# Low weight parts of gate and up, the scale product and sums of squares on VectorE instead of GpSimd

## The chip, the cores and the metric

The kernel runs on one core of one Trainium2 chip. The metric is the device time of one execution in microseconds (us). The core's engines are named as the profile names them: PE is TensorE, DVE is VectorE, ACT is ScalarE, POOL is GpSimd, and SP issues DMAs. PEld is PE's loading of weights, which overlaps its matmuls. Each engine works through its own list of instructions in order; between engines there are semaphores.

## The reference

Two layers of an encoder trunk over 1040 tokens (16 meta tokens and 1024 of the sequence), width 1024, all in float32:

```python
for l in range(DEPTH):                                   # DEPTH = 2
    h = h + hybrid_mixer(rmsnorm(h, norm1_w[l]), ...)    # ends with mix @ w_out
    h = h + swiglu(rmsnorm(h, norm2_w[l]), w_gate_up[l], w_down[l])
h = rmsnorm(h, final_norm_w)

def swiglu(h, w_gate_up, w_down):
    gate, up = jnp.split(h @ w_gate_up, 2, axis=-1)
    return (jax.nn.silu(gate) * up) @ w_down
```

D_FF is 2816, which is 22 tiles of 128 columns. The mixer (a chunked gated delta rule in both directions and a short convolution) is not touched here, apart from the output projection `mix @ w_out` that ends it. rmsnorm needs the sum of squares of h over the 1024 channels for each token, and these sums are gathered while the output projection is being made.

## The kernel before

**Layout.** The residual stream lies channels-first: eight tiles of 128 channels by 1040 tokens. Matmuls take the weights as the stationary operand, 128 by 128, and stream 260 tokens (layer 0, which needs 1040) or 512 tokens (layer 1, which needs only the last 1024).

**Split operands.** To come near float32 with the faster fp32r matmul, every operand is split into a high part, rounded to fp32r by an ACT copy, and a low part, the difference. One product then takes three matmuls: high by high, high by low, low by high (lines 1015 to 1017 in gate and up, 157 to 159 in the plain dense layers, 1435 to 1437 in down). Weights are split on the chip each time: a DMA brings 128x512 raw values, ACT writes `hi` (line 997), and a subtraction writes `lo` (line 998):

```python
def w_op(src, early=False):                                              # L993
    hi, lo = wslot(early)
    ...
    act(out=hi, in_=src, func=AF.Copy)                                   # L997
    ptt(out=lo, in0=src, in1=hi.bitcast(F32), op=ALU.subtract)           # L998
```

`tt` is an elementwise operation of two tensors on DVE, `ptt` the same on POOL. `wslot` hands out seven pairs of buffers in turn, one for each of the products of a round; a pair is free again when PE has ended the product that read it.

**Gate and up.** For each of the 22 tiles f there is one round of the loop at line 1280. It makes a 2x2 block product in the manner of Strassen and Winograd, with seven products in place of eight. Weight operands: A11, A12, A21, A22 are loaded, and four DVE instructions make sums of them (lines 1290, 1291, 1294, 1295), which gives S1 to S4. Each of the seven operands goes through `w_op`. The sums on the side of the tokens (T1 to T4) are made once a layer, with lines 965, 977 and 178. The products p1 to p7 are added up in PSUM banks, and DVE empties these at lines 1314 (p5), 1325 and 1328 (p3, p6), 1332 (p7) and 1341 (p4); ACT empties p1 and p2 (lines 1310 and 1337). Products 5 and 3 share a bank, and so do 6, 7 and 4: the next product may add to the bank only after DVE has read the one before. Layer 0 does each product in two halves of 260 tokens, layer 1 in one of 512. For the first four tiles, the products with A11 and A12 are made early (`early_part`, line 1041), while the output projection ends. At the end of a round the scale of rmsnorm (`rv`, the reciprocal root for each token) is multiplied on, and silu and the product follow:

```python
ptt(out=gv, in0=gv, in1=rv, op=ALU.mult)        # L1355
tt(out=uv, in0=uv, in1=rv, op=ALU.mult)         # L1356
act(out=gv, in_=gv, func=AF.Silu)               # L1357
row_done = tt(out=uv, in0=uv, in1=gv, op=ALU.mult)   # L1358
```

The row goes to DRAM, and sums of rows and of weights for the down stage are prepared in between (lines 1360 and 1364).

**Output projection, second part.** `out_part(z, m)` (line 941) makes the delta-rule half of the projection for channel tile m and token half z, adds it to the residual (line 905, on DVE), and adds the squares to the row of sums: ACT squares (line 949), and line 950 adds. Its weights are split in `wsplit` (line 131) on POOL at this place. When all eight tiles are in, four small matmuls (line 207) sum over the channels.

**Order.** The program is written in plain order with priorities, and a scheduler that keeps a timeline by its own costs arranges each engine's list when the kernel is built. An instruction that changes engine or cost can therefore move others, also on other engines.

Of the kernel before, what the change touches and what calls it, by code (L numbers as in the profile page):

```python
# [7 lines left out]
F32 = mybir.dt.float32  # L8
# [3 lines left out]
ALU = mybir.AluOpType  # L12
# [30 lines left out]
def trunk(ctx: ExitStack, tc: tile.TileContext, xT, w_in, w_ba, w_out, w_gu, w_dn,  # L43
# [21 lines left out]
    def c4k(tag="c"):  # L65
        return sb.tile([128, L], F32, tag="c", bufs=2, name=nm(tag))
# [33 lines left out]
    tt = nc.vector.tensor_tensor  # L100
    stt = nc.vector.scalar_tensor_tensor
    ts = nc.vector.tensor_scalar
    ptt = nc.gpsimd.tensor_tensor
# [29 lines left out]
    def wload(src, nk):  # L133

        res = []
        step = min(nk, WK)
        for k0 in range(0, nk, step):
            kk = min(step, nk - k0)
            hi = wp.tile([128, WK, 128], F32R, tag="whi", name=nm("whi"))
            lo = wp.tile([128, WK, 128], F32R, tag="wlo", name=nm("wlo"))  # L140
            wsplit(src[:, k0:k0 + kk, :], hi[:, 0:kk, :], lo[:, 0:kk, :])
            for k in range(kk):
                res.append((hi[:, k, :], lo[:, k, :]))
        return res

    def dense(ws, xs, chunks, evac, pool=None):

        for (n0, n1) in chunks:
            n = n1 - n0
            ps = (pool or pacc)()  # L150
            K = len(xs)
            here = tc.cur_priority
            if mmp[0] is not None:
                at_prio(mmp[0])
            for k in range(K):
                (wh, wl), (xh, xl) = ws[k], xs[k]
                mm(ps[:, :n], wh, xh[:, n0:n1], start=(k == 0), stop=False)  # L157
                mm(ps[:, :n], wh, xl[:, n0:n1], start=False, stop=False)  # L158
                mm(ps[:, :n], wl, xh[:, n0:n1], start=False, stop=(k == K - 1))  # L159
            if mmp[0] is not None:  # L160
                mmp[0] = tc.cur_priority
                at_prio(here)
            here = tc.cur_priority
            if evp[0] is not None:
                at_prio(evp[0])
            evac(ps[:, :n], n0, n1)
            if evp[0] is not None:
                evp[0] = tc.cur_priority
                at_prio(here)
            for q in (jobs, jobs2, jobs3):  # L170
                f = q.pop(0) if q else None
                if f is not None:
                    f()
# [106 lines left out]
    for l in range(DEPTH):  # L280
# [622 lines left out]
        def add_h(m, then=None):  # L903
            def f(ps, n0, n1):
                tt(out=hr[m][:, n0:n1], in0=ps, in1=hr[m][:, n0:n1], op=ALU.add)
                if then is not None:
                    then(n0, n1)
            return f
# [23 lines left out]
        def half(ap, z):  # L932

            v = ap.rearrange("p (g e) -> p g e", g=4) if len(ap.shape) == 2 else ap.rearrange("p k (g e) -> p k g e", g=4)
            s = slice(1, 3) if z == 0 else slice(0, 4, 3)
            return v[:, s, :] if len(ap.shape) == 2 else v[:, :, s, :]
# [4 lines left out]
        def out_part(z, m):  # L941
            dense(wload(w_out[l, m, :, 0:4, :], 4), os_, hcut[z], add_h(m), pwide)

            v, sv = half(hr[m][:, o0:L], z), half(ss[:, o0:L], z)
            if m == 0:
                act(out=sv, in_=v, func=AF.Square)
            else:
                sq = c4k("sq")[:, 0:NB].rearrange("p (g e) -> p g e", g=2)
                act(out=sq, in_=v, func=AF.Square)
                (ptt if z == 1 and m % 2 == 0 else tt)(out=sv, in0=sv, in1=sq, op=ALU.add)  # L950
            for (n0, n1) in hcut[z]:
                dma(hd[m][:, n0:n1], hr[m][:, n0:n1])

# [39 lines left out]
        def w_op(src, early=False):  # L993
            hi, lo = wslot(early)
            n = src.shape[1]
            hi, lo = hi[:, 0:n, :], lo[:, 0:n, :]
            act(out=hi, in_=src, func=AF.Copy)  # L997
            ptt(out=lo, in0=src, in1=hi.bitcast(F32), op=ALU.subtract)  # L998
            return hi, lo

        bn = [0]
# [278 lines left out]
        for f in range(FT):  # L1280
            A11, A12, A21, A22 = raw4("raw"), raw4("raw"), raw4("ck2"), raw4("ck2")
            dma(A11, w_gu[l, f, 0, :, 0:4, :])
            dma(A21, w_gu[l, f, 1, :, 0:4, :])
            dma(A22, w_gu[l, f, 1, :, 4:8, :])
            dma(A12, w_gu[l, f, 0, :, 4:8, :])
            s1t, s2t = raw4("ck2"), raw4("ck2")
            W = {}
            if f >= NE:
                W["A11"] = w_op(A11)
            tt(out=s1t, in0=A21, in1=A22, op=ALU.add)  # L1290
            tt(out=s2t, in0=s1t, in1=A11, op=ALU.subtract)
            W["S1"] = w_op(s1t)
            W["S2"] = w_op(s2t)
            tt(out=s2t, in0=A12, in1=s2t, op=ALU.subtract)  # L1294
            tt(out=A21, in0=A11, in1=A21, op=ALU.subtract)
            end = f == FT - 1
            for n, a in ([("S3", A21), ("A22", A22), ("S4", s2t), ("A12", A12)] if end else
                         [("S4", s2t), ("S3", A21), ("A12", A12), ("A22", A22)]):
                if f >= NE or n != "A12":
                    W[n] = w_op(a)  # L1300
            adds = s_under(f)
            g, u = early[f] if f < NE else (row((X[1], Y[1])[f % 2] + "f"), row(X[1], F32, 3))
            ps = {}


            def p1(j):
                ps["a", j], ps["c", j], ps["b", j] = pbank(), pbank(), pbank()
                if f >= NE:
                    prod(ps["a", j], W["A11"], T["B11"], j, True)
                    act(out=part(u, 0, j), in_=pin(ps["a", j]), func=AF.Copy)  # L1310

            def p5(j):
                prod(ps["c", j], W["S1"], T["T1"], j, True)
                tt(out=part(u, 1, j), in0=pin(ps["c", j]), in1=part(u, 0, j), op=ALU.add)

            def p3(j):
                prod(ps["c", j], W["S4"], T["B22"], j, False)
                (gadd if end else gset)(ps["c", j], j)

            def p6(j):  # L1320
                prod(ps["b", j], W["S2"], T["T2"], j, True)
                (gset if end else gadd)(ps["b", j], j)

            def gset(p, j):
                tt(out=part(g, 1, j), in0=pin(p), in1=part(u, 0, j), op=ALU.add)

            def gadd(p, j):
                tt(out=part(g, 1, j), in0=pin(p), in1=part(g, 1, j), op=ALU.add)

            def p7(j):  # L1330
                prod(ps["b", j], W["S3"], T["T3"], j, False)
                tt(out=part(u, 1, j), in0=pin(ps["b", j]), in1=part(u, 1, j), op=ALU.add)

            def p2(j):
                if f >= NE:
                    prod(ps["a", j], W["A12"], T["B21"], j, False)
                    act(out=part(g, 0, j), in_=pin(ps["a", j]), func=AF.Copy)

            def p4(j):
                prod(ps["b", j], W["A22"], T["T4"], j, False)  # L1340
                tt(out=part(u, 0, j), in0=pin(ps["b", j]), in1=part(u, 0, j), op=ALU.add)

            p1_ = (p1, p6, p7)
            if end:

                for p in (p1, p5, p6, p7, p4, p3, p2):
                    for j in range(NJ):
                        p(j)
                    down_begins(p)
            else:  # L1350
                for j in range(NJ):
                    for p in (p1, p5, p3, p6, p7, p2, p4):
                        p(j)
            gv, uv, rv = g[:, o0:L], u[:, o0:L], ss[:, o0:L]
            ptt(out=gv, in0=gv, in1=rv, op=ALU.mult)  # L1355
            tt(out=uv, in0=uv, in1=rv, op=ALU.mult)  # L1356
            act(out=gv, in_=gv, func=AF.Silu)  # L1357
            row_done = tt(out=uv, in0=uv, in1=gv, op=ALU.mult)  # L1358
            for to, r, o in adds:
                after(tt(out=to, in0=r, in1=o, op=ALU.add), row_done if f < FT - 1 else row_before)  # L1360
            row_before = row_done
            dma(ad[f][:, o0:L], uv)
            if NF <= f < NF + NP:
                tt(out=gv[:, 0:NB].rearrange("p (g e) -> p g e", g=2), in0=half(uv, 1), in1=half(uv, 0), op=ALU.subtract)
                dma(td[f - NF], gv[:, 0:NB])
# [45 lines left out]
        for u, (p, b, m) in enumerate(UNITS):  # L1411
            if b == 1 and p in FIRST:
                dh, z = FIRST[p]
# [14 lines left out]
            for j in range(NJ):  # L1428
# [9 lines left out]
                if b == NBK - 1:  # L1438
                    dh, z, op = TO[p]
# [11 lines left out]
        else:  # L1451
# [22 lines left out]
            for (n0, n1) in FIN:  # L1474
                e = (n1 - n0) // 4
                sv = ss[:, n0:n1]
# [6 lines left out]
                for m in range(KT):  # L1483
# [4 lines left out]
                    else:  # L1488
                        summed(sv, True, False)
                        sq = c4k("sq")[:, 0:n1 - n0]  # L1490
# [87 lines left out]
```

## Time and profile before

| what | value |
|---|---|
| runs of the kernel before | 2550.4, 2552.06, 2552.34 us (median 2552.06) |
| profiled execution: span from first to last instruction | 2550.9 us |
| mean granted PE clock | 0.996 |
| PE busy | 2489.1 us, 98% |
| DVE busy | 1636.6 us, 64% |
| ACT busy | 1045.7 us, 41% |
| POOL busy | 1135.7 us, 45% |

The profile gives one execution; for it there is the span and no other time, and the span lies inside the range of the three runs. In the groups of instructions a row reads: line, engine, operation, what it writes and reads with buffer numbers left out, shape, count; then busy us, mean ns of one, and the idle time of the engine just before them with what ended it. In the rows of waits stand the us in total, how often, and the longest. Rows with three figures joined by strokes give the shortest, the median and the longest duration in ns. The tiles appear under the tags of their buffers, so `whi`, `wlo`, `a` and `b` may all be weight parts, and `rw` and `raw` are raw weights and their sums. Gate and up with the early part of it fills about 580 to 1065 us in layer 0 and 1845 to 2310 us in layer 1.

### The profile page before, as it was taken

How to read it: one execution, taken by the hardware profiler on the slowest of the kernel's cores; microseconds unless marked ns; L12 is line 12 of the kernel's file. 1: busy time of each engine (PE TensorE's matmuls, PEld its weight loads, DVE VectorE, ACT ScalarE, POOL GpSimd, SP SyncE). 2: the span in 40 equal slices, each digit the busy share in tenths (PEclk: the TensorE clock that was granted, in tenths of full speed). 3: DMA queues.
4: the chain of work that ended last, by engine and by line, in shares of the span. 5: the costliest groups of instructions: out<-in, count | busy, mean ns of one | idle time of the engine just before them, and what ended most of it. 6: DMA issues, size and time to landing. Idle time of an engine off the chain costs nothing. (4 is left out here: it accounts for less than half of the span.)

```text
span 2550.9 us, 45282 instructions
## 1 busy us (share of the span) xinstructions
PE 2489.1 (98%) x17508; PEld 2277.7 (89%) x17508; DVE 1636.6 (64%) x2547; ACT 1045.7 (41%) x1944; POOL 1135.7 (45%) x885
## 2 busy tenths in 40 slices
PE   8999999998999999999999999999989999999998
PEld 6989999998999999999999888998968778777787
DVE  4788233749766655767657892335687777558664
ACT  5554333535233333344445543334443333234444
POOL 2131212525666666655411212233557666575662
PEclk9999999999999999999999999999999999999999
DMA  3445253633223322764224443446332233328641
GB/s 129 135 158 169 100 167 125 202 93 119 97 101 103 108 92 85 236 204 136 92 81 144 148 159 108 156 129 201 121 118 91 95 107 103 100 94 273 189 121 66
DMA packets 199531, 335.27 MB, mean 131 GB/s; under 512 B 23404, under 2 KB 85668, under 8 KB 199316
## 3 DMA queue, kind: packets, MB, share of 16 engines
q1 hardware_dynamic: 171204, 293.84, 35.6%
q10 hardware_dynamic: 25936, 34.19, 4.1%
q0 software_dynamic: 2176, 4.36, 0.6%
q8 instruction: 137, 2.24, 0.4%
q14 instruction: 78, 0.64, 0.1%
HBM read 250.31 MB, written 81.99 MB: 130 GB/s over the span
## 5 line engine op out<-in xcount | busy, mean ns | idle before, releaser
L131 POOL TENSOR_TENSOR wlo<-raw,whi 128x512 fp32r<-128x512 f32 x132 | 177.7, 1348 | 661.2 <-ACT whi L130 538.0
L157 PE MATMUL pacc<-a,whi 128*128 128x346 f32 (+1 forms) x808 | 263.7, 329 | 8.0 <-ACT whi L130 7.7
L159 PE MATMUL pacc<-a,wlo 128*128 128x346 f32 (+1 forms) x808 | 262.3, 326 | 0.9 <-DVE wlo L131 0.5
L157 PE MATMUL pacc<-b,whi 128*128 128x346 f32 (+2 forms) x672 | 233.6, 348 | 2.5 <-ACT b L900 1.8
L159 PE MATMUL pacc<-b,wlo 128*128 128x346 f32 (+2 forms) x672 | 232.7, 348 | 0.8 <-DVE wlo L131 0.8
L158 PE MATMUL pacc<-a,whi 128*128 128x346 f32 (+1 forms) x688 | 224.9, 327 | 0.0
L158 PE MATMUL pacc<-b,whi 128*128 128x346 f32 (+2 forms) x580 | 200.3, 345 | 0.0
L130 ACT ACTIVATE whi<-raw 128x512 fp32r<-128x512 f32 x168 | 106.0, 631 | 224.1 <-PE pacc L158 119.0
L998 POOL TENSOR_TENSOR wlo<-rw,whi 128x512 fp32r<-128x512 f32 x92 | 133.8, 1456 | 74.8 <-ACT whi L997 73.5
L157 PEld LDWEIGHTS pacc<-a,whi 128*128 128x128 f32 x808 | 152.2, 189 | 13.8 <-ACT whi L130 8.1
L159 PEld LDWEIGHTS pacc<-a,wlo 128*128 128x128 f32 x808 | 152.6, 189 | 2.0 <-POOL wlo L131 0.7
L157 PEld LDWEIGHTS pacc<-b,whi 128*128 128x128 f32 x672 | 126.5, 188 | 14.4 <-issue 3.1
L159 PEld LDWEIGHTS pacc<-b,wlo 128*128 128x128 f32 x672 | 126.3, 188 | 9.7 <-DVE wlo L131 1.0
L158 PEld LDWEIGHTS pacc<-a,whi 128*128 128x128 f32 x688 | 130.0, 189 | 3.0 <-issue 1.9
L998 POOL TENSOR_TENSOR a<-rw,a 128x512 fp32r<-128x512 f32 x64 | 105.8, 1655 | 57.2 <-ACT a L997 56.2
L998 POOL TENSOR_TENSOR b<-rw,b 128x512 fp32r<-128x512 f32 x64 | 91.1, 1427 | 85.2 <-ACT b L997 59.8
L997 ACT ACTIVATE whi<-rw 128x512 fp32r<-128x512 f32 x92 | 57.8, 630 | 147.0 <-DVE rw L1294 76.7
L158 PEld LDWEIGHTS pacc<-b,whi 128*128 128x128 f32 x580 | 109.2, 188 | 7.0 <-issue 0.4
L997 ACT ACTIVATE b<-rw 128x512 fp32r<-128x512 f32 x64 | 40.1, 630 | 128.6 <-PE pacc L1016 32.3
L1290 DVE TENSOR_TENSOR rw<-rw,rw 128x512 f32<-128x512 f32 x44 | 61.4, 1395 | 45.6 <-POOL wlo L998 25.4
L296 DVE TENSOR_TENSOR a<-pacc,rstd 128x346 f32<-128x346 f32 (+2 forms) x59 | 32.6, 554 | 89.4 <-PE pacc L159 89.1
L998 POOL TENSOR_TENSOR wlo<-raw,whi 128x512 fp32r<-128x512 f32 x50 | 73.3, 1468 | 31.7 <-ACT whi L997 25.1
(967 smaller groups left out, 8439.8 us busy)
## 6 DMA issues: line engine op xcount, KB each, us to landing
raw<-in_w_in SPq DMA_DIRECT2D x112, 256.0 KB, 2.7
raw<-in_w_gu SPq DMA_DIRECT2D x104, 256.0 KB, 2.7
rw<-in_w_gu SPq DMA_DIRECT2D x88, 256.0 KB, 3.1
rw<-in_w_dn SPq DMA_DIRECT2D x94, 192.0 KB, 2.5
rec<-vkd SPq DMA_DIRECT2D x61, 256.0 KB, 2.8
raw<-in_w_out SPq DMA_DIRECT2D x48, 256.0 KB, 2.5
b<-ad SPq DMA_DIRECT2D x45, 260.0 KB, 3.4
a<-ad SPq DMA_DIRECT2D x45, 256.0 KB, 4.1
```

Of the source, the lines that this page charges most:

```text
L130: whi_done[0] = act(out=hi, in_=raw[:, 0:kk, :], func=AF.Copy)
L131: (tt if lov[0] else ptt)(out=lo, in0=raw[:, 0:kk, :], in1=hi.bitcast(F32), op=ALU.subtract)
L157: mm(ps[:, :n], wh, xh[:, n0:n1], start=(k == 0), stop=False)
L158: mm(ps[:, :n], wh, xl[:, n0:n1], start=False, stop=False)
L159: mm(ps[:, :n], wl, xh[:, n0:n1], start=False, stop=(k == K - 1))
L296: tt(out=t[:, n0:n1], in0=ps, in1=rstd[:, n0:n1], op=ALU.mult)
L997: act(out=hi, in_=src, func=AF.Copy)
L998: ptt(out=lo, in0=src, in1=hi.bitcast(F32), op=ALU.subtract)
L1290: tt(out=s1t, in0=A21, in1=A22, op=ALU.add)
```

## The change

Three places take `tt` in place of `ptt`, so the instruction goes into DVE's list instead of POOL's. Operands, shapes and results are the same. The first place had one of the two engines by turns: of the sums for the second token half, those of tiles 2, 4 and 6 were on POOL.

```diff
@@ out_part
                 act(out=sq, in_=v, func=AF.Square)
-                (ptt if z == 1 and m % 2 == 0 else tt)(out=sv, in0=sv, in1=sq, op=ALU.add)
+                tt(out=sv, in0=sv, in1=sq, op=ALU.add)
@@ w_op
             act(out=hi, in_=src, func=AF.Copy)
-            ptt(out=lo, in0=src, in1=hi.bitcast(F32), op=ALU.subtract)
+            tt(out=lo, in0=src, in1=hi.bitcast(F32), op=ALU.subtract)
             return hi, lo
@@ end of a round of gate and up
-            ptt(out=gv, in0=gv, in1=rv, op=ALU.mult)
+            tt(out=gv, in0=gv, in1=rv, op=ALU.mult)
             tt(out=uv, in0=uv, in1=rv, op=ALU.mult)
             act(out=gv, in_=gv, func=AF.Silu)
```

In the built program 308 instructions of line 998, 44 of line 1355 and 6 of line 950 stand on DVE instead of POOL. The splits of the down weights (line 1197) and of the output projection's weights (line 131) stay on POOL. The scheduler arranges the lists of PE, DVE and ACT anew in the stretch from the second half of the output projection to the first part of the down stage, in both layers.

## The prediction

> **What bounds the kernel now.** I read the page's busy times first, then a table of stretches around the two gate-and-up stages, then who PE waited for there, then the durations of the operations concerned, and last one short timeline.
>
> ```profile
> span 2550.9 us, 45282 instructions
> ...
> PE 2489.1 (98%) x17508; PEld 2277.7 (89%) x17508; DVE 1636.6 (64%) x2547; ACT 1045.7 (41%) x1944; POOL 1135.7 (45%) x885
> core 0: us, PE busy (x) PEld busy (x) DVE busy (x) ACT busy (x) POOL busy (x), PEclk, DMA share, GB/s
> 560.00:640.00 80.00, 72.59 (x582) 69.53 (x580) 69.38 (x84) 41.95 (x74) 44.36 (x30) 1.00 0.44 134
> 640.00:1040.00 400.00, 391.81 (x3229) 388.29 (x3230) 256.48 (x343) 129.29 (x224) 255.78 (x156) 1.00 0.29 96
> 1845.00:1910.00 65.00, 53.76 (x270) 43.38 (x270) 56.21 (x59) 31.35 (x49) 35.77 (x25) 0.96 0.39 124
> 1910.00:2290.00 380.00, 374.19 (x1603) 301.69 (x1602) 255.25 (x235) 120.75 (x192) 252.27 (x155) 0.99 0.29 98
> ```
>
> PE is the bound: 98% of the span. The change can pay only where PE stands still in these stretches, and that is little. Length less PE busy gives 7.4 and 8.2 us in layer 0, 11.2 and 5.8 us in layer 1: 33 us in all, 14.0 of it in the two long steady stretches (640 to 1040, 1910 to 2290), 18.6 in the two start-ups. The built order of the changed kernel differs on PE, DVE and ACT only from the second half of the out-projection to the first part of the down stage, in both layers; so I charge nothing elsewhere.
>
> Who PE waited for, the first row from layer 0, the others from layer 1 (waited for: us in total, times, longest):
>
> ```profile
> PE pacc L1015 <- DVE a L1332: 3.6, 9, 0.4
> PE pf L1015 <- DVE b L1332: 4.3, 4, 1.8
> PE pacc L157 <- ACT whi L130: 3.4, 1, 3.4
> PE pa L1015 <- DVE a L1328: 3.2, 1, 3.2
> PE pa L207 <- DVE rstd L950: 3.1, 1, 3.1
> PE pacc L1015 <- DVE b L1332: 1.5, 1, 1.5
> ```
>
> Most of these end on DVE, and mostly on one instruction: L1332, which empties the bank of product 7 before product 4 may add into it. PE is almost never held by a low part itself. So the question is not how long a low part takes but when DVE gets round to L1332.
>
> **What makes DVE late.** Minimum, median and maximum duration in ns of four DVE groups, then of the GpSimd ones that move:
>
> ```profile
> L131 DVE TENSOR_TENSOR wlo<-raw,whi x36: 616/684/759, 78.4 to 1481.8; 128x512 fp32r<-128x512 f32 x36
> L1332 DVE TENSOR_TENSOR b<-pacc,b x7: 676/678/692, 1927.8 to 2275.1; 128x512 f32<-128x512 f32 x7
> L1290 DVE TENSOR_TENSOR rw<-rw,rw x44: 675/1596/2886, 466.3 to 2269.3; 128x512 f32<-128x512 f32 x44
> L1356 DVE TENSOR_TENSOR b<-b,rstd x21: 1211/2132/2185, 1922.8 to 2321.6; 128x1024 f32<-128x1024 f32 x21
> L998 POOL TENSOR_TENSOR wlo<-rw,whi x92: 1279/1296/2298, 622.1 to 2286.9; 128x512 fp32r<-128x512 f32 x92
> L1355 POOL TENSOR_TENSOR b3f<-b3f,rstd x19: 2417/2853/3372, 689.2 to 2288.2; 128x1040 f32<-128x1040 f32 x10, 128x1024 f32<-128x1024 f32 x9
> L950 DVE TENSOR_TENSOR rstd<-rstd,sq x22: 674/702/1755, 554.4 to 1876.5; 128x520 f32<-128x520 f32 x11, 128x512 f32<-128x512 f32 x11
> ```
>
> L1332 and L1290 have the same size. L1332 reads one operand from PSUM and never exceeds 0.69 us; L1290 reads both from SBUF, can take 0.675 us too, but has a median of 1.6 and goes to 2.9. GpSimd's splits do the same: 1.28 us at best, 2.3 at worst. In the timeline of layer 1 (start, duration) the slow ones can be watched beside GpSimd's work (its L1355 is the last row):
>
> ```profile
> 2163.44 0.69 DVE L1341 TENSOR_TENSOR b<-pb,b 128x512 f32<-128x512 f32 x1 [1.56 <-PE pb L1017]
> 2164.17 2.15 DVE L1356 TENSOR_TENSOR b<-b,rstd 128x1024 f32<-128x1024 f32 x1
> 2166.35 2.20 DVE L1358 TENSOR_TENSOR b<-b,a3f 128x1024 f32<-128x1024 f32 x1
> 2168.48 2.88 DVE L1290 TENSOR_TENSOR rw<-rw,rw 128x512 f32<-128x512 f32 x1
> 2171.29 1.65 DVE L1360 TENSOR_TENSOR a<-S 128x384 f32<-128x384 f32 x1
> 2172.86 1.77 DVE L1295 TENSOR_TENSOR rw<-raw,rw 128x512 f32<-128x512 f32 x1
> 2174.55 0.68 DVE L1332 TENSOR_TENSOR b<-pf,b 128x512 f32<-128x512 f32 x1
> 2167.44 3.37 POOL L1355 TENSOR_TENSOR b3f<-b3f,rstd 128x1024 f32<-128x1024 f32 x1
> ```
>
> Five instructions take 10.4 us from 2164.17 to L1332. At the undisturbed 1.21 us for the two wide and at most 0.69 for the three others they would take 4.5. The Trainium skill, page "SBUF — State Buffer", section "Who interferes with whom", states this as a rule: a VectorE instruction with two SBUF inputs and a GpSimd instruction that reads SBUF exclude each other, and the second waits for the whole of the first. The trace agrees (0.675 against a median of 1.6 us; PSUM operand never over 0.69).
>
> **The change part by part.** *Low parts and scale product, steady stretch of layer 1 (380 us).* What leaves GpSimd there, first and last group of four at L998 (134 instructions in all), and the first of three at L1355 (21); then DVE's disturbed groups in the same stretch:
>
> ```profile
> L998 POOL TENSOR_TENSOR b<-rw,b 128x512 fp32r<-128x512 f32 x58 | 82.6, 1425 | 83.3 <-ACT b L997 58.0 <-PE pacc L1017 12.1 <-PE pf L1017 9.3
> L998 POOL TENSOR_TENSOR wlo<-raw,whi 128x512 fp32r<-128x512 f32 x17 | 26.1, 1534 | 4.4 <-ACT whi L997 4.4
> L1355 POOL TENSOR_TENSOR b3f<-b3f,rstd 128x1024 f32<-128x1024 f32 x9 | 25.5, 2835 | 2.3 <-DVE b3f L1328 2.3
> L1356 DVE TENSOR_TENSOR b<-b,rstd 128x1024 f32<-128x1024 f32 x19 | 37.3, 1964 | 0.7
> L1295 DVE TENSOR_TENSOR rw<-raw,rw 128x512 f32<-128x512 f32 x19 | 36.5, 1921 | 0.5
> L1290 DVE TENSOR_TENSOR rw<-rw,rw 128x512 f32<-128x512 f32 x19 | 25.8, 1356 | 19.5 <-DMA rw<-in_w_gu 11.0 <-POOL wlo L998 7.1 <-POOL b L998 1.4
> L1291 DVE TENSOR_TENSOR rw<-rw,raw 128x512 f32<-128x512 f32 x19 | 22.8, 1198 | 6.2 <-POOL b L998 6.2
> L1294 DVE TENSOR_TENSOR rw<-raw,rw 128x512 f32<-128x512 f32 x20 | 18.0, 902 | 20.2 <-POOL b L998 17.8 <-POOL wlo L998 2.3
> ```
>
> Added on DVE: 134 x 0.684 us (L131 is the same operation, done on DVE) + 21 x 1.21 = 117 us. Taken off, since GpSimd then runs nothing in this stretch: 19 x 0.75 (L1356) + 19 x 1.23 (L1295) + 19 x 0.67 + 19 x 0.51 + 20 x 0.21 = 64 us. DVE goes from 255 to at most 308 us of 380, 81%; L1358, L1360 and L1364, disturbed too, would lower it further. The waits of L1290, L1291 and L1294 for GpSimd (35 us) go as well: the buffer is then released by DVE's own earlier instruction.
>
> New is that DVE, in order, now waits for ScalarE's high part before a low part, with the bank emptyings queued behind and PE behind those. In the built order only 6 of the 308 low parts stand directly behind the DVE sum that they split; the rest have other work between. I price such a wait at 0.9 us, an estimate from the high part's own time and half as much for its two hand-overs, and a wait with one or two instructions between at 0.3:
>
> ```profile
> L997 ACT ACTIVATE whi<-rw x92: 612/632/635, 620.8 to 2286.2; 128x512 fp32r<-128x512 f32 x92
> ```
>
> 6 x 0.9 and some 30 x 0.3 are 14 us over 44 rounds, far inside DVE's idle time (72 us are left in this stretch alone). Between L1341 and L1332, the place above, the built order has one low part more in its short cases: 4.5 + 0.7 us in place of 10.4, and the wait of 1.5 us there goes.
>
> So of the 14.0 us that PE idles in the steady stretches I take two thirds away (the rows for L1332 shown carry 9.4): -9 us. Bounds: all of it, -14; or new lateness, +15 at 0.4 us for each of 38 rounds.
>
> *Start-ups.* There DVE is nearly full (69.4 of 80, 56.2 of 65 us). Of GpSimd's 30 instructions in layer 0's start-up only these stay on it:
>
> ```profile
> L131 POOL TENSOR_TENSOR wlo<-raw,whi 128x512 fp32r<-128x512 f32 x10 | 14.2, 1416 | 18.8 <-ACT whi L130 18.8
> ```
>
> The other 20, 17 low parts and 3 sums of squares, add 20 x 0.69 = 14 us to DVE; where each had disturbed one DVE instruction it gives back L950's 1.755 - 0.674 = 1.08 us, and I take it for two in three: -14. Together 0, with ends at -8 (the 3.1 us wait for L950 and the 3.2 for L1328 go in layer 1, some in layer 0) and +12 (the sums for T2 and T4 stand behind low parts that wait for buffers which PE has yet to release). The six L950 themselves are in this.
>
> *Sum.* Span 2550.9 - 9 = 2542; the shown runs have a median 1.1 us over this span, so 2543.
>
> **The rivals.** *A, slower: DVE's order becomes the bound.* A low part whose high part waits for PE to free a weight buffer holds the bank emptyings behind it, and PE stands at product 4 or 3. For it speaks DVE at 81% in order; against it, that PE releases a weight buffer long before the next round's product needs it: a round takes 20 us (380 us over 19 L1356), so a product 2.9, and six products lie between, 17 us in layer 1 and, with its two halves, half of that in layer 0. It decides from the point where L1332 comes over 2.8 us (layer 0: 24 matmuls in the built order, 392 us over 3229 each) after product 7. At 1 us for each of 40 rounds: +40, 2592; at a third of that, +13, 2565. *B, no difference:* the work only changes place, DVE's disturbed 64 us against 117 added, and PE was hardly waiting: 2548 to 2556. The Trainium skill, page "Perfetto Trace Analysis", section "Optimizing Scalar/DVE Operations", says that since the two share a read port, moving work between them might not help; by that rule alone the sum would be 0. *C, faster than forecast:* start-ups gain their 8 too and all steady waits go: 2530. *D, the change does not do what it says:* excluded, since the built order has 308 L998, 44 L1355 and 6 L950 more on DVE and as many fewer on GpSimd.
>
> **How the numbers follow.** Forecast with C (2528 to 2547) 0.47; B 0.20; A 0.33, of which about a third beyond 2575. Range 2528 to 2575: below lie the few cases where over 24 of the 33 idle us go, above the far end of A. The forecast without C has a range of its own of 2534 to 2547. What a measurement of this kernel can tell is about 0.2%, 5 us.
>
> **What would show it.** Right: in both long stretches POOL empty, DVE 75 to 81%, L1290 and L1295 at a mean under 0.75 us, L1332 no longer first among PE's waits, PE idle there under 6 us. Wrong: PE idle above 14 us there, with L1314, L1328 or L1332 as releasers and DVE waiting for ACT at L998 before them (rival A); or PE idle in the two start-ups well over 19 us.

## The result, and the profile after

The changed kernel takes 2519.6 us (median of 4 runs, 2515.5 to 2521.6) against 2552.2 us for the kernel before beside it (4 runs, 2550.4 to 2552.8): a ratio of 0.9879, with a 95% interval of 0.9866 to 0.9892. That is 32.6 us less. The forecast was 2543, and its range ended at 2528: the direction was right, the size was not.

The head of the page of after, and the table of stretches. Its rows are cut where the work lies now: layer 0's long stretch ends 10 us earlier than before's; layer 1's start-up and long stretch begin 25 us earlier, and the latter is 5 us shorter.

```profile
span 2517.8 us, 44947 instructions
...
PE 2478.8 (98%) x17508; PEld 2276.3 (90%) x17508; DVE 1679.0 (67%) x2905; ACT 1044.1 (41%) x1944; POOL 564.1 (22%) x527
```

```profile
core 0: us, PE busy (x) PEld busy (x) DVE busy (x) ACT busy (x) POOL busy (x), PEclk, DMA share, GB/s
560.00:640.00 80.00, 77.07 (x626) 75.66 (x625) 70.74 (x114) 45.86 (x78) 12.96 (x10) 0.98 0.45 143
640.00:1030.00 390.00, 390.00 (x3253) 390.00 (x3253) 297.15 (x496) 129.09 (x230) 5.62 (x5) 1.00 0.29 99
1820.00:1885.00 65.00, 61.47 (x353) 51.93 (x352) 59.94 (x88) 35.51 (x56) 9.17 (x6) 1.00 0.42 140
1885.00:2260.00 375.00, 374.45 (x1616) 302.88 (x1615) 276.59 (x395) 124.30 (x197) 4.45 (x5) 1.00 0.30 101
```

First, POOL is nearly empty in the long stretches (5.6 and 4.5 us). Second, VectorE took over all that work and is still busy for only 297 of 390 and 277 of 375 us (76% and 74%). In the start-up of layer 0 it does 114 instructions in 70.7 us, where it did 84 in 69.4. Third, the matmul counts say more than PE's busy time. Before, PE was shown busy for 391.8 of 400 us in layer 0, a loss of 8.2; but it did 3229 matmuls there, 0.1239 us each, against 0.1199 each after. At after's pace those 3229 take 387 us, so 13 us were lost, not 8. The ends of matmuls are modelled: in layer 0 each is shown with 0.28 us at a spacing of 0.12, so a wait shorter than the overlap does not appear as idle time.

The gain is therefore counted in what follows by the number of the matmul, which does not depend on where a window is cut. Gate and up is 3696 matmuls in layer 0 and 1848 in layer 1 (L1015 to L1017 in order of start, all in the trace of every run). The start-up is the time from the start of the first to that of number 351 and 181; the middle is the next 3200 and 1580. These times are worked out from the records of the trace, one execution of each kernel; other durations come from the views. The last column runs from the start of a layer's first matmul to that of its last.

| us | start-up 0 | middle 0 | start-up 1 | middle 1 | all gate and up |
|---|---|---|---|---|---|
| before | 60.7 | 395.1 | 65.0 | 373.0 | 933.6 |
| after | 54.0 | 383.8 | 53.1 | 367.1 | 898.9 |
| difference | -6.7 | -11.3 | -11.9 | -5.9 | -34.7 |

All of the gain lies in gate and up (the ends and the other stages add 1 to 2 us back), and a little over half of it in the start-ups.

The groups on DVE that were disturbed, and the moved ones (minimum, median, maximum in ns):

```profile
L998 DVE TENSOR_TENSOR wlo<-rw,whi x92: 678/684/695, 616.0 to 2251.7; 128x512 fp32r<-128x512 f32 x92
L1355 DVE TENSOR_TENSOR b3f<-b3f,rstd x19: 1218/1233/1237, 680.7 to 2252.3; 128x1040 f32<-128x1040 f32 x10, 128x1024 f32<-128x1024 f32 x9
L1290 DVE TENSOR_TENSOR rw<-rw,rw x44: 627/686/1751, 466.4 to 2233.8; 128x512 f32<-128x512 f32 x44
L1295 DVE TENSOR_TENSOR rw<-raw,rw x44: 679/685/692, 617.2 to 2236.6; 128x512 f32<-128x512 f32 x44
L1356 DVE TENSOR_TENSOR b<-b,rstd x21: 1212/1218/2028, 1897.8 to 2287.3; 128x1024 f32<-128x1024 f32 x21
```

L1290's median fell from 1.596 to 0.686 us and L1356's from 2.132 to 1.218. The low part costs 0.684 us where POOL needed 1.296. In the timeline of layer 1 the sequence shown of before, from an L1356 to an L1332, now looks like this (start, duration):

```profile
2133.62 1.22 DVE L1356 TENSOR_TENSOR b<-b,rstd 128x1024 f32<-128x1024 f32 x1
2134.76 0.69 DVE L1290 TENSOR_TENSOR rw<-rw,rw 128x512 f32<-128x512 f32 x1
2135.36 0.68 DVE L998 TENSOR_TENSOR wlo<-raw,whi 128x512 fp32r<-128x512 f32 x1
2135.96 1.22 DVE L1358 TENSOR_TENSOR b<-b,a3f 128x1024 f32<-128x1024 f32 x1
2137.10 1.22 DVE L1355 TENSOR_TENSOR b3f<-b3f,rstd 128x1024 f32<-128x1024 f32 x1
2138.23 0.69 DVE L1295 TENSOR_TENSOR rw<-raw,rw 128x512 f32<-128x512 f32 x1
2138.83 0.55 DVE L1360 TENSOR_TENSOR a<-S 128x384 f32<-128x384 f32 x1
2139.30 0.69 DVE L1332 TENSOR_TENSOR b<-pf,b 128x512 f32<-128x512 f32 x1
```

The same five instructions and two more, a low part and a scale product, take 5.7 us where the five alone took 10.4. PE's waits for DVE have nearly gone. Its first waits in layer 0's start-up and middle (560 to 1040 us), then DVE's two longest for ScalarE at the low parts over the whole span (us, times, longest):

```profile
PE pf L1015 <- ACT whi L997: 1.7, 1, 1.7
PE pa L1015 <- ACT whi L997: 0.5, 1, 0.5
PE pb L1015 <- ACT a L1051: 0.5, 1, 0.5
PE pacc L1015 <- DVE a L1332: 0.4, 1, 0.4
```

```profile
DVE a L998 <- ACT a L997: 14.2, 28, 1.1
DVE b L998 <- ACT b L997: 12.8, 14, 1.9
```

### The profile page after: what moved, and what is told of

It is laid out like the page before. It is cut to its first block, busy times and chain, and to the rows that moved or that the text cites. A ratio compares the mean times of both kernels' runs of the same rounds, so it can differ in the third digit from the quotient of the medians.

```text
span 2517.8 us, 44947 instructions
## 1 busy us (share of the span) xinstructions
PE 2478.8 (98%) x17508; PEld 2276.3 (90%) x17508; DVE 1679.0 (67%) x2905; ACT 1044.1 (41%) x1944; POOL 564.1 (22%) x527
## 5 line engine op out<-in xcount | busy, mean ns | idle before, releaser
L131 POOL TENSOR_TENSOR wlo<-raw,whi 128x512 fp32r<-128x512 f32 x132 | 177.8, 1349 | 668.2 <-ACT whi L130 539.4
L130 ACT ACTIVATE whi<-raw 128x512 fp32r<-128x512 f32 x168 | 106.0, 631 | 225.5 <-PE pacc L158 121.3
L1197 POOL TENSOR_TENSOR b<-b,b 128x384 fp32r<-128x384 f32 x11 | 13.8, 1271 | 438.1 <-ACT b L1196 438.1
L1197 POOL TENSOR_TENSOR a<-a,a 128x384 fp32r<-128x384 f32 x11 | 11.9, 1092 | 418.8 <-ACT a L1196 418.8
L296 DVE TENSOR_TENSOR a<-pacc,rstd 128x346 f32<-128x346 f32 (+2 forms) x59 | 32.6, 554 | 89.4 <-PE pacc L159 89.1
L296 DVE TENSOR_TENSOR b<-pacc,rstd 128x346 f32<-128x346 f32 (+1 forms) x63 | 32.5, 515 | 82.4 <-PE pacc L159 82.3
L997 ACT ACTIVATE a<-rw 128x512 fp32r<-128x512 f32 x64 | 40.1, 629 | 102.0 <-PE pacc L1016 60.3
L1245 DVE TENSOR_TENSOR P<-a,P 128x512 fp32r<-128x512 f32 x63 | 61.8, 1008 | 25.1 <-ACT P L1244 24.7
```

Source lines behind the costliest of these rows:

```text
L130: whi_done[0] = act(out=hi, in_=raw[:, 0:kk, :], func=AF.Copy)
L131: (tt if lov[0] else ptt)(out=lo, in0=raw[:, 0:kk, :], in1=hi.bitcast(F32), op=ALU.subtract)
L296: tt(out=t[:, n0:n1], in0=ps, in1=rstd[:, n0:n1], op=ALU.mult)
L1197: ptt(out=lo, in0=r, in1=hi.bitcast(F32), op=ALU.subtract)
L1245: behind(tt(out=lo, in0=r, in1=hi.bitcast(F32), op=ALU.subtract))
```

## The experiments

The theory: GpSimd's instructions that read SBUF hold up VectorE's instructions with two SBUF operands, VectorE then empties banks and adds up late, and PE waits. The rivals: the work merely got faster because VectorE does it in half the time; or the waits for GpSimd's results, and not its reading, had made VectorE late; or the scheduler's new lists are better. In the recorded expectations theory P is the first, theory O a gain by the shorter path or the new lists. All ratios are against runs of the kernel before on the same chip in the same sitting. The last four columns are the matmul times defined above.

| run | us | ratio, 95% interval | start-up 0 | middle 0 | start-up 1 | middle 1 |
|---|---|---|---|---|---|---|
| lo_only | 2523.2 | 0.9900, 0.9883 to 0.9917 | 53.4 | 383.9 | 57.9 | 367.1 |
| scale_only | 2540.3 | 0.9968, 0.9955 to 0.9981 | 60.9 | 385.1 | 62.4 | 366.1 |
| dummy_read | 2557.8 | 1.0032, 1.0020 to 1.0045 | 61.5 | 383.8 | 68.6 | 366.3 |
| dummy_write | 2520.3 | 0.9885, 0.9871 to 0.9900 | 53.8 | 383.8 | 56.4 | 366.7 |
| steady_part | 2528.4 | 0.9916, 0.9893 to 0.9939 | 57.9 | 383.8 | 60.7 | 366.3 |
| early_part | 2538.8 | 0.9949, 0.9931 to 0.9967 | 53.6 | 396.1 | 54.5 | 376.2 |
| down_too | 2516.8 | 0.9863, 0.9847 to 0.9879 | 53.6 | 383.8 | 54.1 | 366.6 |
| out_too | 2514.7 | 0.9851, 0.9835 to 0.9866 | 50.4 | 383.8 | 52.3 | 366.3 |
| tied_read | 2548.0 | 0.9987, 0.9978 to 0.9996 | 60.3 | 384.3 | 59.3 | 374.7 |
| tied_write | 2520.8 | 0.9878, 0.9863 to 0.9892 | 54.1 | 383.8 | 54.2 | 367.0 |
| down_out_too | 2510.9 | 0.9845, 0.9829 to 0.9861 | 50.4 | 383.8 | 52.5 | 366.3 |
| quiet | 2507.7 | 0.9826, 0.9811 to 0.9840 | 50.4 | 383.8 | 53.1 | 366.3 |
| sums_only | 2543.2 | 0.9968, 0.9955 to 0.9981 | 57.8 | 393.6 | 61.0 | 373.7 |
| early_low | 2541.1 | 0.9962, 0.9950 to 0.9973 | 55.0 | 397.9 | 57.2 | 376.0 |
| tied_scale | 2561.2 | 1.0042, 1.0029 to 1.0055 | 62.6 | 389.0 | 61.4 | 379.9 |
| tied_wait | 2571.7 | 1.0087, 1.0071 to 1.0103 | 58.5 | 406.5 | 56.0 | 380.7 |

### Parts of the change: low parts alone, scale product alone

```diff
 lo_only      # line 998 alone
-            ptt(out=lo, in0=src, in1=hi.bitcast(F32), op=ALU.subtract)
+            tt(out=lo, in0=src, in1=hi.bitcast(F32), op=ALU.subtract)
 scale_only   # line 1355 alone
-            ptt(out=gv, in0=gv, in1=rv, op=ALU.mult)
+            tt(out=gv, in0=gv, in1=rv, op=ALU.mult)
```

> Only the low parts (L998) move to VectorE; the scale product (L1355) and the sums of squares stay on GpSimd. Theory P (GpSimd instructions that read SBUF hold up VectorE's two-operand ones, and VectorE late holds up PE): L998 is 460 us of the 590 us of GpSimd work that the change takes away, so about 78% of the 32.6 us: 2552 - 25 = 2527 us. Theory O (the gain comes from the low part's shorter path and the scheduler's new lists, not from the engines disturbing each other): all of it, 2520 us, since the low part carries the path.

> Only the scale product (L1355) moves. Theory P: 120 of 590 us of disturbing work goes, and each piece is the longest single one (2.8 us): -6 to -10, 2542 to 2546 us. Theory O: no low part is touched, 2550 to 2552 us.

The low parts bring 25.9 us and the scale product 8.8 (against 2549.1 in this sitting), together 34.7 and about the whole. Both are what theory P had named (25, and 6 to 10). Yet its sharing out by amount of GpSimd work is not what the stages show, for there they do not add up: each alone brings the middles to 384 to 385 and 366 to 367, the level of the whole change. The middles are lost only while both kinds of work are on GpSimd. Most of the start-ups' gain comes with the low parts; the sums of squares are in neither run.

scale_only says more. GpSimd is still busy for 208 of 380 us in layer 1's long stretch, nearly all of it with low parts; L1290 still has a median of 1.746 us over both layers, and L1294 waits 23.5 us for low parts in that stretch (17.8 before), while L1295 is back at 0.679 (1.773 before). PE loses nothing in this:

```profile
1910.00:2290.00 380.00, 380.00 (x1642) 307.79 (x1641) 269.16 (x266) 125.11 (x200) 208.42 (x141) 1.00 0.33 107
```

So a DVE that is lengthened in part and waits need not hold up PE. Nor does the order of before's lists: in layer 0's middle 2601 of the 3200 matmuls of scale_only write and read the tiles that stand at the same place of before's list, and 10.0 of the 11.3 us are gained.

### Parts of the change by place: rounds and early part

```diff
 steady_part  # line 998, with line 1355 on DVE and line 950 as before
+            (ptt if early else tt)(out=lo, in0=src, in1=hi.bitcast(F32), op=ALU.subtract)
 early_part   # line 998, with line 950 on DVE and line 1355 as before
+            (tt if early else ptt)(out=lo, in0=src, in1=hi.bitcast(F32), op=ALU.subtract)
```

> The low parts of the rounds proper (292 of 308) and the scale product move; the 16 early low parts and the sums of squares stay on GpSimd, so the start-ups are as before. Counted by matmuls per us, the steady stretches lost 21 us to waiting (12.9 in layer 0, 8.0 in layer 1), and the rest of the 33 is start-up. Theory P: -21 to -26, 2526 to 2531 us. If the start-ups gave nothing, as the prediction booked them: 2519 to 2522 us.

> The opposite half: only the 16 early low parts and the six sums of squares move. Theory P, start-ups worth some 10 us: 2539 to 2545 us. Start-ups worth 0, as booked: 2549 to 2553 us. VectorE, nearly full there, overloaded: over 2553 us.

The rounds bring 23.5 us and the early part, 22 instructions that the forecast had booked at nothing, brings 13.0. The middle of early_part stays where it was before, or 1 to 3 us above it; its whole gain lies in the start-ups. Against its expectation, steady_part shortens the start-ups too, by 2.8 and 4.3 us: the first rounds lie in them.

### What carries the start-ups

```diff
 sums_only    # line 950 alone
-                (ptt if z == 1 and m % 2 == 0 else tt)(out=sv, in0=sv, in1=sq, op=ALU.add)
+                tt(out=sv, in0=sv, in1=sq, op=ALU.add)
 early_low    # line 998 alone, as in early_part
+            (tt if early else ptt)(out=lo, in0=src, in1=hi.bitcast(F32), op=ALU.subtract)
```

> Only the six sums of squares (L950) on VectorE; low parts and scale product stay on GpSimd. What is counted here and in the next three is the time from the start of one gate-and-up matmul to the start of another, by their number: 1 to 351 of 3696 in layer 0 and 1 to 181 of 1848 in layer 1 are the start-ups (before 60.7 and 65.0 us, after 54.0 and 53.1), the next 3200 and 1580 the middle (before 395.1 and 373.0, after 383.8 and 367.1). If the start-ups' gain is that of the 16 early low parts, the sums bring no more than layer 1's one wait of 3.1 us for L950: 2547 to 2550 us, start-ups 60 to 61 and 61 to 62. If it hangs on the sums, which end the out-projection: 2540 or less, start-ups 54 to 56 in both.

> Only the 16 early low parts (two for each of four row tiles in two layers) on VectorE; the sums of squares, the 292 low parts of the rounds and the scale product stay on GpSimd. If the early low parts carry the start-ups: start-up of layer 0 at 53.4 as with all low parts moved, layer 1 at 57 to 59, middle as before (395, 373), 2538 to 2543 us. If they need the sums beside them: over 2545.

The expectation for the sums was a miss: six instructions brought 6.8 us (against 2550.0), 2.9 and 4.0 of them in the two start-ups; I had given them one wait of 3.1 us at most. The 16 low parts brought 8.9 us in all: 5.7 and 7.8 in the start-ups, less some 3 us in each layer's middle. Neither carries the start-ups alone. The stretch 580 to 640 us in before, early_low and sums_only, in this order:

```profile
580.00:640.00 60.00, 52.59 (x415) 49.53 (x413) 55.21 (x58) 30.05 (x55) 35.37 (x23) 1.00 0.37 117
```

```profile
580.00:640.00 60.00, 56.75 (x451) 54.94 (x450) 55.48 (x75) 33.16 (x58) 22.78 (x16) 0.97 0.42 129
```

```profile
580.00:640.00 60.00, 54.01 (x428) 52.19 (x426) 57.31 (x66) 31.25 (x57) 31.05 (x20) 0.97 0.38 119
```

In early_low DVE (the third busy time) does 17 more instructions than in before in about the same busy time, 55.5 against 55.2 us, and PE does 36 more matmuls. Where DVE is nearly full, an early low part on GpSimd took from it about what the same work costs on it.

### Reading or writing: extra GpSimd work that nobody needs

Four kernels add to the changed kernel work on GpSimd on a scratch tile that nothing else reads. The first two are not tied to anything:

```diff
 dummy_read   # in w_op, after the buffers are handed out; dummy_write: two nc.gpsimd.memset(scr, 0.0)
+            ptt(out=scr, in0=scr, in1=scr, op=ALU.mult)
+            ptt(out=scr, in0=scr, in1=scr, op=ALU.mult)
```

> The changed kernel, and beside every low part two GpSimd products of 128x256 on a scratch tile of their own, which nobody waits for; the output is the same. Theory P: GpSimd is as busy as before and reads SBUF, VectorE's two-operand instructions are held up again, now with the low parts among them: 2545 to 2590 us. Theory O: nobody waits for the dummy, 2518 to 2524 us.

> As dummy_read, but the two GpSimd instructions are memsets of the scratch tile, which write SBUF and read nothing. If it is GpSimd's reading that disturbs: 2518 to 2524 us, as the changed kernel. If any GpSimd work on SBUF does: near dummy_read, over 2535 us. Theory O: 2518 to 2524 us.

As a test of the rounds both fail: GpSimd had no reason to wait and did the whole work ahead; that 2557.8 us lies in theory P's range is luck. In the row of dummy_read for layer 0's middle POOL (the sixth figure) is busy for 0.8 of 400 us:

```profile
640.00:1040.00 400.00, 399.52 (x3327) 398.32 (x3327) 311.24 (x518) 136.41 (x239) 0.82 (x1) 1.00 0.32 103
```

What is left of it is that the reads, done from 255 us on, cost 37 us against the memsets, 17 of it before gate and up begins (its first matmul starts at 605.2 and 588.3 us) and 20 in the two start-ups, where POOL was now busy (73 of 80 us in layer 0's, 15 with the memsets). That is not the price of reading alone: a product has a median of 0.615 us and a memset 0.312, so the reads also fill GpSimd's list for longer, and ScalarE's high parts of the projection weights (L130) waited 30.8 us for the products against 18.2 for the memsets. The two others are therefore tied to the ScalarE copy that makes the high part, and so lie where the low parts lay:

```diff
 tied_read    # tied_write: four nc.gpsimd.memset(scr, 0.0) in place of the two products
-            act(out=hi, in_=src, func=AF.Copy)
+            split = act(out=hi, in_=src, func=AF.Copy)
+            for _ in range(2):
+                after(ptt(out=scr, in0=scr, in1=scr, op=ALU.mult), split)
             tt(out=lo, in0=src, in1=hi.bitcast(F32), op=ALU.subtract)
```

> As dummy_read, but each pair of GpSimd products on the scratch tile now waits for the ScalarE high part of its own round, so that it runs inside gate and up, when the low part did before; nobody waits for it, the output is the same, and the lists of PE and VectorE are those of the changed kernel but for about 60 of 16500 rows. Theory P: VectorE, which now carries the low parts as well, is held up by 1.2 us of GpSimd reading at a time: two-operand instructions longer than 1 us in the mean, 2545 to 2600 us. Theory O: 2518 to 2524 us.

> As tied_read, with four GpSimd memsets of the scratch tile (about 1.25 us together, as long as the two products) in place of the products: GpSimd as busy at the same places, writing SBUF and reading nothing. If it is the reading that holds VectorE up: 2518 to 2524 us and VectorE's two-operand instructions at 0.69 us. If any GpSimd work does: as tied_read.

The reads cost 27 of the 33 us gained, the writes nothing. The middle of layer 1, first with reads and then with writes:

```profile
1910.00:2290.00 380.00, 374.75 (x1608) 302.39 (x1607) 342.02 (x389) 123.17 (x198) 281.52 (x273) 1.00 0.31 104
```

```profile
1885.00:2260.00 375.00, 374.55 (x1617) 302.92 (x1616) 276.71 (x395) 123.53 (x196) 171.23 (x542) 1.00 0.30 101
```

DVE does the same work, some 390 instructions, in 342 us beside reads and in 277 beside writes. What one instruction shows of this, the low part on DVE (line 1003 here) and the added work, tied_read and then tied_write:

```profile
L1003 DVE TENSOR_TENSOR wlo<-raw,whi x50: 678/1096/1105, 587.0 to 2255.9; 128x512 fp32r<-128x512 f32 x50
L1002 POOL TENSOR_TENSOR scr<-scr x616: 603/942/1709, 584.9 to 2290.6; 128x256 f32<-128x256 f32 x154
```

```profile
L1003 DVE TENSOR_TENSOR wlo<-raw,whi x50: 676/684/693, 587.6 to 2234.3; 128x512 fp32r<-128x512 f32 x50
L1002 POOL MEMSET scr<- x1232: 305/312/507, 585.8 to 2269.1; 128x256 f32 x176
```

The low part's median is 1.096 us beside reads and 0.684 beside writes, and the reads themselves rise from 0.603 to a median of 0.942. By stages the reads bring back 6.3 of the 6.7 us of layer 0's start-up, 6.2 of layer 1's 11.9, and more than the 5.9 of its middle; but of the 11.3 us of layer 0's middle only 0.5, although DVE is lengthened there as well (351 of 400 us busy). The lists do not account for it: in the start-ups and middles every matmul of tied_read and of tied_write writes and reads the tiles that stand at the same place of after's list. So tied_read has all the moved work on VectorE and after's list on PE, and yet gains only 2.8 us over before: the new lists are not the gain, nor is a shorter path for the low part by itself, since 1.096 us is still less than the 1.296 on GpSimd.

Two limits. POOL is busy for longer with the reads (282 against 171 us in the rows shown), so that work still on it, the out-projection's low parts in the start-ups and the down stage's, could wait longer. And DVE carries the low parts here, so PE stands at other places than in before: of its waits in layer 0's start-up that tied_write does not have, the longest end on DVE, at the low parts (tied_write has 0.2 us there):

```profile
PE pacc L1022 <- DVE wlo L1003: 1.8, 1, 1.8
...
PE pacc L1022 <- DVE a L1003: 1.2, 1, 1.2
```

### Layer 0's middle: the reading, or the waits for its results

```diff
 tied_scale   # tied_read, and line 1355 back on GpSimd
 tied_wait    # tied_write, and waits for the memsets
-            tt(out=s1t, in0=A21, in1=A22, op=ALU.add)
+            after(tt(out=s1t, in0=A21, in1=A22, op=ALU.add), pw[0])       # L1290: last memset of the round before
-            tt(out=s2t, in0=A12, in1=s2t, op=ALU.subtract)
+            after(tt(out=s2t, in0=A12, in1=s2t, op=ALU.subtract), pm[0])  # L1294: last memset of S2
-            tt(out=gv, in0=gv, in1=rv, op=ALU.mult)
-            act(out=gv, in_=gv, func=AF.Silu)
+            scaled = tt(out=gv, in0=gv, in1=rv, op=ALU.mult)
+            for _ in range(9):
+                pm[0] = after(nc.gpsimd.memset(scr, 0.0), scaled)
+            after(act(out=gv, in_=gv, func=AF.Silu), pm[0])
```

> The changed kernel with the scale product back on GpSimd (as in lo_only, whose middles are 383.9 and 367.1) and the two tied reads of 0.94 us for each low part (as in tied_read, whose middles are 384.3 and 374.7). No VectorE sum waits for GpSimd, but the Silu on ScalarE waits for the scale product, which queues behind the reads. If the middle of layer 0 is lost by reading alone, once there is as much of it as before: 392 or more, and 2550 us or more. If by ScalarE's wait for the scale product in GpSimd's queue: 390 or more, with L1357's wait for L1355 first among ScalarE's waits. If it needs VectorE's sums waiting for low parts on GpSimd: 386 or less, and about 2548 us as with tied_read.

> The changed kernel with waits for GpSimd put back and no reading by it: four memsets tied to each high part, as in tied_write, and nine tied to each scale product (2.8 us, the length of the product on GpSimd); L1290 waits for the memsets of the round before's last operand, L1294 for those of S2's, and the Silu for the nine. If reading alone costs the time: as tied_write, 2518 to 2524 us, middles 384 and 367. If the waits for GpSimd cost layer 0's middle: 390 or more there, 2528 us or more, with PE waiting for L1332 again.

Neither came out as one theory alone had it. More reading, with no sum on DVE waiting for GpSimd, brought back 5.2 of the 11.3 us (389.0, between the two bounds named), but the Silu waited 8.1 us for the scale product there. tied_wait, with no reading, cost more than before's whole loss: 406.5 against 395.1. In tied_wait the sums are not lengthened (a median of 0.691 us at line 1296, which is L1290's place), but they wait, and PE is held by the high parts made from them (middle of layer 0):

```profile
DVE rw L1296 <- POOL scr L1002: 20.4, 15, 1.4
```

```profile
PE pacc L1020 <- ACT whi L1000: 9.9, 10, 1.0
PE pb L1020 <- ACT whi L1000: 4.0, 4, 1.0
```

In before, the same sum waited about as long there for GpSimd's low parts, and the Silu for its scale product (the row is one of three, 40.1 us together; 6.7 in tied_wait):

```profile
DVE rw L1290 <- POOL wlo L998: 18.3, 13, 1.6
...
DVE rw L1291 <- POOL a L998: 6.6, 13, 0.8
```

```profile
ACT b3f L1357 <- POOL b3f L1355: 17.5, 9, 6.1
```

This does not show that the waits alone cost the time, for the scheduler also built tied_wait in another order. In layer 0's middle 2887 of its 3200 matmuls write or read other tiles than those at the same place of after's list, where tied_write has none. DVE and ACT empty the two halves of a product side by side in a steady round of tied_wait (products 4 4 5 5 1 3 6 3 6 2 7 2 7 1), where after has other products between them (5 4 3 2 6 1 5 7 3 6 2 4 7 1). And PE was held by L1332 in before and by the high parts in tied_wait. So what held PE in before's middle of layer 0, reading, waiting or both, stays open; the scale product beside the low parts on GpSimd is a condition of it, as lo_only and scale_only show. tied_wait is also 13.7 us over tied_write in layer 1's middle, where DVE's L1300 (L1294's place) waits 38.0 us for GpSimd against 17.8 before; there too its other order (1244 of 1580 matmuls) keeps the waits from being priced.

### Onward: the rest of GpSimd's work

```diff
 down_too     # line 1197, the down weights' low parts
-ptt(...)
+tt(...)
 out_too      # line 131 from the out-projection's second part on
+        lov[0] = True
 down_out_too # both
 quiet        # both, and lines 857 and 929 (attention's subtractions) on DVE
```

> The changed kernel, and the 168 low parts of the down weights (L1197, 128x384, some 1.25 us each on GpSimd) go to VectorE too. L1245 there still has a mean of 0.92 to 1.01 us where 0.69 is possible, and PE spacing in the first part of the down stages loses about 13 us in both layers. Theory P: up to half of that, 2513 to 2518 us. If PE waits there for weights and DMAs rather than for VectorE: 2518 to 2522 us. If VectorE, 0.55 us more for each of 168, gets late: over 2523 us.

> The changed kernel, and the low parts of the weights from the second part of the output projection on (L131: those and the few plain rows of down) go to VectorE too. Theory P: the last GpSimd readers leave the start-ups, where VectorE is busy 71 of 80 and 60 of 65 us: some of the 10 us that PE still loses there goes, 2513 to 2519 us. If VectorE is simply full there, each of 16 low parts costs its 0.65 us: 2520 to 2530 us.

> The changed kernel with the further low parts of down_too and out_too both on VectorE. If the gains add (3 and 5 us against the 2519.6 of the changed kernel): 2510 to 2514 us. If they are the same waiting twice: 2514 to 2517 us.

> As down_out_too, and the two GpSimd products of the end of the scan (L857) and the low parts of the mixer's output (L929), 16 and 24 instructions, on VectorE too. Theory P: some disturbed VectorE instructions less in the scan, whose steps are chains of VectorE and PE, 0 to -4 us beside down_out_too. If GpSimd's parallel work is needed there: +2 to +8 us.

The down stage's low parts alone can't be told from the changed kernel (the intervals overlap). The out-projection's stand at the edge (the intervals meet at 0.9866; the runs of out_too, up to 2515.4, lie just below the change's, from 2515.5). Both together gain what the two gain singly, as the first expectation for down_out_too had it, and the last is the fastest version: 2507.7 us, 43 below the kernel before beside it (2550.9), a ratio of 0.9826 where the change had 0.9879. out_too shortens layer 0's start-up by 3.6 us more (54.0 to 50.4): with the out-projection's low parts gone from it, POOL stands empty there, and PE does 656 matmuls from 560 to 640 us, against 626 after and 582 before:

```profile
560.00:640.00 80.00, 79.04 (x656) 77.72 (x655) 76.00 (x131) 47.76 (x79) 0.00 (x0) 1.00 0.51 152
```

DVE now does 131 instructions in those 80 us and is busy for 76.0, and PE is not held up by that.

## Why the prediction was right or wrong, point by point

**What held PE** was named rightly as far as it went. POOL is nearly empty in both long stretches; DVE stands at 76% and 74% (75 to 81 forecast, so just under it in layer 1); L1290 and L1295 have means of 0.68 to 0.69 us there (under 0.75 forecast); L1332 fell from the first of PE's waits to one of 0.4 us; PE's idle time there is 0.6 us (under 6 forecast). These signs held, or nearly, while the time was out, so they could not tell a gain of 9 from one of 17. Tied reads lengthen DVE's instructions and bring back most of the time, tied writes neither, with the same list on PE: that GpSimd's reading is enough for such a loss is shown in the start-ups and in layer 1's middle. That it was the whole of before's loss there is not shown: sums on DVE waited for GpSimd in before as well, and scale_only has such reading and waiting in layer 1's middle without a loss.

**The step that failed most: the start-ups at 0.** They gave 18.6 us by matmul number. (That PE's idle time there in before was also 18.6 is chance; 6.5 us of idle time remain after.) The step had counted DVE's load, 14 us added and 14 taken off, and concluded that nothing changes. The count was not far off (DVE's busy time in layer 0's start-up rose by 1.4 us, with 44 more matmuls done in the same 80 us), but it does not answer the question. What counts there is when the work that PE stands at gets through, not how full DVE is: in layer 1, PE waited 3.1 us at L207 for the sums (L950) in before, 1.1 in sums_only, and not at all after. That a chain of out-projection, sums and early low parts is what paces the start-ups is my reading of such rows; no run isolates it. The gain has two parts, 6.9 us from six sums and 13.5 from sixteen low parts when each is done alone; the far end of -8 held less than half of it.

**The second: 14.0 us as all that the middles could give, and two thirds of it taken.** They gave 17.2 us where -9 was booked. The bound was length less PE busy, and that hides every wait shorter than the overlap of the modelled matmuls. Counted by matmuls per us against after's pace, which only the result gave, the steady loss was 21 us: 3229 matmuls at 0.1239 - 0.1199 us are 13 us in layer 0, and 1603 at 0.2371 - 0.2321 are 8 in layer 1 (that is above 17.2 in part because those windows begin some 57 and 22 matmuls earlier than the middles). Taking two thirds rested on L1332's listed waits being most of it; all of it went. With both terms at their measured size the sum is 2550.9 - 35.8 = 2515.1, and the span was 2517.8.

**In layer 0's middle the mechanism stays open.** It gave 11.3 us, nearly as much as layer 1's start-up. Reading at the places of the low parts alone brought back 0.5 of it. The waits of DVE's sums for GpSimd's results (35 us in layer 1) were named in the prediction, but no term of the sum was theirs, and the Silu's wait was not named. tied_wait, with such waits and no reading, lost 22.7 us there, but in another order of products.

**The waits of DVE's list at the low parts** for ScalarE's high parts were put at 14 us, and the two rows above and one of 4.3 us for `whi` make 31. They were rightly held harmless: DVE has 93 and 98 us left in the two middles.

**The rivals.** A, DVE's order as the bound, did not come, not even with 131 instructions in 80 us of start-up. B, no difference, did not come either. The Trainium skill, page "Perfetto Trace Analysis", section "Optimizing Scalar/DVE Operations", says that offloading work between the two engines might not help; read as a gain of 0, this is not what these runs show: taking such work back gained 1.2%. C had the right sign for every stage, with the start-ups at 8 where they measured 18.6. The Trainium skill, page "SBUF — State Buffer", section "Who interferes with whom", also states that a GpSimd instruction that only writes does not disturb VectorE's two-input instructions. The runs agree: the tied memsets leave the low part at 0.684 us.

## What to carry to other kernels

Price a helper engine by what it takes from the others, not by its own idle time: here a subtraction that takes 0.68 us on VectorE took 1.3 us on GpSimd, lengthened what VectorE did meanwhile, and made sums and copies wait for its result. Where an engine looks 98% busy with pipelined work, count its instructions per us in the disturbed and in an undisturbed stretch before bounding a gain by its idle time. And a start-up in which a second engine is nearly full is the first place to look, not one to book at zero because the loads balance. Where a scheduler makes the lists, compare them before an added wait is priced: tied_wait put a large part of PE's work in another order.

## What the runs showed of the hardware that I had not expected

The lengthening is mutual: GpSimd's product of 256 columns takes 0.603 us at least and 0.942 in the median beside a busy VectorE, and VectorE's low part goes from 0.684 to 1.096 us beside it, each by half to two thirds of the other's shortest duration. Memsets on GpSimd at 171 of 375 us busy left VectorE's time for the same work unchanged (276.7 against 276.6 us). And how busy VectorE is did not tell whether PE would wait: in layer 0's middle PE kept its pace of 0.12 us for a matmul with VectorE idle for 93 of 390 us (after) and for 49 of 400 (tied_read), and lost 11 us with 144 of 400 idle (before).
